# Layer 1's matrices into the states, built from loads that spread the input matrices and the turned powers over the partitions

## The chip, the cores and the metric

The kernel runs on one core of one Trainium2 chip. The metric is device time in microseconds (us), the median of several executions. One further execution was profiled; its trace is what the prediction reads.

## The reference, cut to what matters

Two layers of an encoder run over 256 tokens of width 1024. In each layer a normed input is projected to ten column groups; one branch is a bidirectional state-space model, two are attention, and the gated branches are projected back and added to the input. The change touches only the state-space branch, and in it only the matrices that carry a group's 16 input channels into its 64 complex states.

```python
for direction in range(2):
    lam_bar = exp(lam * dt)                       # per group (32) and state (64)
    b_bar = ((lam_bar - 1) / lam)[..., None] * b  # b is complex, (group, state, channel)
    bu = einsum('gpc,bsgc->bsgp', b_bar, u)
    h = scan(h[s] = lam_bar * h[s-1] + bu[s])     # direction 1 runs backwards
    y += einsum('gcp,bsgp->bsgc', c, h).real
```

The kernel cuts the 256 steps into 64 chunks of T = 4. A chunk's entry into the state is then one product: for step t of the chunk the matrix is b times the power of lam_bar that is left until the chunk's end. (The factor (lam_bar - 1) / lam is put on c instead.) So for each layer 128 rows (two directions x 64 states) x 32 groups x 16 channels x 4 steps of complex products b * q have to be formed, q being the four powers. On TensorE the contraction runs over (channel, step), so these must stand on the partitions, while powers and states are computed with (direction, state) on the partitions.

## The kernel before, in words

All work is written as streams (Python generators). A stream names the engine of its next step, the buffers that it needs and the events that it waits for. A planner (class Flow) keeps a modelled clock for each engine, gives every instruction a modelled cost, and always emits the step that can start first by its model, less a "patience" of its stream, with a "rank" to break ties. What comes out is one fixed order of instructions on each engine. The chip keeps that order: an instruction that waits holds back all that stand behind it on its engine. The planner's clocks run through the whole program, so a change in one step can give a different order of everything behind it, while what was emitted before it stays as it was.

SyncE (SP) issues nearly all DMAs, from one queue in the planned order. The weights come in pieces of 512 KB: load_pieces (L474) loads one into one of three raw slots, high_parts (L484) casts it on ScalarE (or VectorE) to whi (three slots), low_parts (L498) subtracts on VectorE to wlo (two slots), which frees the raw slot, and TensorE multiplies: 24 matmuls with 256 columns for a piece (run_layer, L1409, and mm3, L378). A raw load waits in SP's queue for its slot, and wlo waits for TensorE to be done with the piece two before. Almost every instruction is recorded under line 135, that of the planner's wrapper, so the names of the tiles tell the steps apart. If the planner sees a gap on TensorE, keep_warm (L432) lets it put small matmuls on an identity ("warm") there.

For each layer, ssm_params (L662) loads the parameters (layer 1 must wait for the slot "tab", which layer 0 holds until its last convolution matrices are computed), ssm_tables (L673) builds the powers pw and from them q1 (the four powers, in turned order for the backward direction), and ssm_into (L760) makes for each of four batches of eight groups the products wt on VectorE, five instructions of 512 elements per partition. into_turn (L788) then turns them: two groups of four TensorE transposes into a bank psw of PSUM ("sm", two banks for all small users), each followed by a ScalarE copy to wb. ssm_x (L803) multiplies wb with the inputs u into psx. Behind the end of layer 0 the norm, the splitting of the normed input and, through DRAM, the tiles xa, xad and u of layer 1 precede its first psx.

to_mix (L1249) is the step of layer 0 and 1 that gates the state-space output on VectorE (sg, mo, mix2) ahead of the last output products. DMA costs in the planner (L175): 0.475 us to issue (0.65 when a source with under 64 rows spreads over 128 partitions), 0.65 us to start, the bytes at 360 GB/s one DMA after another, 0.85 us to land.

Of the kernel before, what the change touches and what calls it, by code (L numbers as in the profile page):

```python
# [12 lines left out]
F32 = mybir.dt.float32  # L13
# [7 lines left out]
P = 128  # L21
# [5 lines left out]
HD = 64  # L27
GROUPS = 32
NST = 64
CH = 16  # L30
T = 4
# [3 lines left out]
NB = GROUPS // GB  # L35
N1 = NCH + 1
RS = GROUPS * N1
PAIRS = GB // 2
# [17 lines left out]


SLOTS = dict(raw=3, whi=3, wlo=2, act=3, qkv=6, g4=7, wb=4, tm=3, E=1, u=5, bias=2, t2k=2, pt=2, ptt=2,
            xa=1, sg=5, bd=1, bs=1, rs=1, ys=3, tab=1, atn=1, pj=3, sc=2, po=1, sm=2)

PLAIN = ((0, 1, 2, 3, 5, 8), (0, 1))

BY_DMA = (0, 0)

EARLY = (2, 1)
FILL = 0.9
# [18 lines left out]
            keep_x=(2.7, 8.1), pair=(2.5, 0.5), head=(2.5, 0.5), gelu=(9.0, 0.2), to_mix=(5.2, 1.4), to_x=(7.4, 1.4), load_pieces=1.5,  # L85
            into_turn=(0.1, 5.1), t5_rows=(1.9, 5.1), biases=(5.2, 7.9), reload_x=(1.3, 4.3),
            bias_glu=(8.7, 6.0), ssm_x=(3.8, 7.6), ssm_scan=(6.7, 3.1), ssm_kernels=(5.2, 4.9), ssm_y=(3.7, 3.6),
            ssm_up=(3.8, 3.1), ssm_tables=(2.1, 7.5), ssm_into=5.0, ssm_out=(0.8, 5.3), products=(5.2, 1.2))

BACKLOG = 4  # L90

# [12 lines left out]
def ap(base, offset, dims):  # L104
    return bass.AP(base.tensor, base.offset + offset, dims)


def free(t, offset, dims):

    return bass.AP(t.tensor, t.offset + offset, [t.ap[0]] + dims)  # L110
# [3 lines left out]
class Event:  # L114
    t, eng = None, None
# [225 lines left out]
def trunk(ctx: ExitStack, tc: tile.TileContext, io):  # L341
    nc = tc.nc
    flow = Flow(tc)
    V, A, G, PE, SP = flow.V, flow.A, flow.G, flow.PE, flow.SP

    sb = ctx.enter_context(tc.tile_pool(name="sb", bufs=1))
    dram = ctx.enter_context(tc.tile_pool(name="dram", bufs=2, space=DRAM))
    psum = ctx.enter_context(tc.tile_pool(name="psum", bufs=1, space=PSUM))

    def new(tag, dims, dtype=F32, name=None):  # L350

        return sb.tile([P] + dims, dtype, name=name or tag, tag=tag, bufs=SLOTS[tag])

    def bank(tag, name=None):
        return psum.tile([P, 512], F32, name=name or tag, tag=tag, bufs=SLOTS[tag])
# [1 line left out]
    def one(name, dims, dtype=F32, bufs=1):  # L357
        return sb.tile([P] + dims, dtype, name=name, tag=name, bufs=bufs)
# [28 lines left out]
    def events(n):  # L387
        return [Event() for _ in range(n)]
# [22 lines left out]
    ident, ones, epst = one("ident", [P]), one("ones", [1]), one("epst", [1])  # L411
    eye16, namask, fg = one("eye16", [CH]), one("namask", [2, NEAR]), one("fg", [KD])
    bd = one("bd", [2, GB, CH, 2])
# [259 lines left out]
    def ssm_tables(l, tb):  # L673

        G1 = GROUPS
# [8 lines left out]
        def rows(dst, first):  # L684
            A.copy(dst[:NST], pw[:NST, :, first:first + T, :])
            s = pw[NST:]
            A.copy(dst[NST:], free(s, (first + T - 1) * G1, [[STEP, 2], [-G1, T], [1, G1]]))

        for base, n in ((0, 1), (0, 2), (3, 1), (4, 1), (4, 2)):
            i = base + n  # L690
            yield "V", "tm"
            pt = new("tm", [2, 2, 2, G1], name="pt")
            pt1, pt2 = pt[:, 0], pt[:, 1]
            src = pw[:, :, base + 1:base + n + 1, :]
            V.tensor_mul(pt1[:, :, :n, :], src, free(pw, i * G1, [[0, 2], [0, n], [1, G1]]))
            yield "V"
            V.tensor_mul(pt2[:, :, :n, :], swapped(pw, (base + 1) * G1, STEP, [[G1, n], [1, G1]]),
                         free(pw, STEP + i * G1, [[0, 2], [0, n], [1, G1]]))
            yield "V"
            V.tensor_sub(pw[:, 0, i + 1:i + n + 1, :], pt1[:, 0, :n, :], pt2[:, 0, :n, :])  # L700
            V.tensor_add(pw[:, 1, i + 1:i + n + 1, :], pt1[:, 1, :n, :], pt2[:, 1, :n, :])
            flow.free("tm")
            if base == 0 and n == 2:

                yield "A"
                q1 = one("q1", [2, G1, T])
                rows(q1.rearrange("p r g t -> p r t g"), 0)
                q1sd = one("q1sd", [2, G1, T])
                yield "V"
                V.tensor_sub(q1sd[:, 0], q1[:, 0], q1[:, 1])  # L710
                V.tensor_add(q1sd[:, 1], q1[:, 0], q1[:, 1])
                tb.q1, tb.q1sd = q1, q1sd
                yield "V", tb.par_ev
                tb.bsum = one("bsum", [GROUPS, CH])
                V.tensor_add(tb.bsum, tb.bb[:, 0], tb.bb[:, 1])
                flow.set(tb.q1_ev)
# [39 lines left out]
        V.tensor_add(csum, cc[:, 0], cc[:, 1])  # L756
        tb.qc, tb.qsd, tb.csum = qc, qsd, csum
        flow.set(tb.ev)

    def ssm_into(l, tb):  # L760

# [258 lines left out]
    def ssm_start(l):  # L1020
        tb = Box()
        tb.wb, tb.wc, tb.toep, tb.y_left = [None] * NB, [], [None] * NB, NB
        tb.tab_ev, tb.par_ev, tb.q1_ev, tb.l_ev, tb.ev, tb.scan_ev, tb.wcs_ev = events(7)
        tb.into_ev, tb.x_ev, tb.wc_ev, tb.toep_ev = events(NB), events(NB), events(NB), events(NB)
        flow.spawn(ssm_params(l, tb), l)
        flow.spawn(ssm_tables(l, tb), l)
        flow.spawn(ssm_into(l, tb), l)
        return tb

    def ssm_run(L, tb):  # L1030
# [605 lines left out]
def layout(x, norm_g, w_in, w_out, ssm_lam_re, ssm_lam_im, ssm_log_dt, ssm_b_re, ssm_b_im, ssm_c_re, ssm_c_im,  # L1636
           ssm_d, glu_w, glu_b, na_rpb, t5_bias, final_g):
    a = {k: np.asarray(v) for k, v in locals().items()}
    L, G = DEPTH, GROUPS
    o = {}  # L1640
# [5 lines left out]
    w = a["w_in"]  # L1646
    w = np.concatenate([w[:, :, _SPLIT[i]:_SPLIT[i + 1]][:, :, pm if i == 1 else slice(None)] for i in _ORDER], axis=2)
# [11 lines left out]
    b = np.stack([a["ssm_b_re"], a["ssm_b_im"]], 1)  # L1659
    c = np.stack([a["ssm_c_re"], a["ssm_c_im"]], 1)  # L1660
    o["b_p"] = b.transpose(0, 2, 4, 1, 3, 5).reshape(L, P, 2, G, CH)
    o["c_p"] = c.transpose(0, 2, 5, 1, 3, 4).reshape(L, P, 2, G, CH)
    d = a["ssm_d"].reshape(L, 8, 4, CH)
    d = np.broadcast_to(d[..., None], (L, 8, 4, CH, 2))
# [22 lines left out]
```

## Time and profile before

| | us |
|---|---|
| Median of 3 executions | 459.48 (458.31 to 461.18) |
| The profiled execution | 457.03 |
| Its span, first to last instruction | 455.2 |
| TensorE busy | 444.5 (98%) |
| VectorE busy | 349.6 (77%) |
| ScalarE busy | 301.5 (66%) |
| DMA engines, mean share | 52% |

The span is what the trace covers; 1.8 us of the profiled execution lie around it. Busy time of TensorE counts pipelined matmuls, so it says that the engine had work, and the pace of the matmuls says how fast that went.

### The profile page before, as it was taken

The page shows a single profiled execution, that of the slowest core. Times are in us where ns is not written, and L with a number is a line of the kernel's source. Part 1 is how long each engine was busy: PE and PEld are TensorE (multiplying, and loading weights), DVE is VectorE, ACT ScalarE, POOL GpSimd, SP SyncE. Part 2 cuts the span into 40 slices and gives each one's busy share as a digit, 9 for nine tenths or more (in the row PEclk, how much of TensorE's full clock was granted, in tenths as well). Part 3 has the DMA queues.
Part 4 walks back from the last instruction along what each step waited for, and adds up shares of the span by engine and source line. Part 5 has one row for each costly group of instructions (what it writes and reads, how often), then busy time and mean ns, then how long its engine had stood idle before and what let it go on. Part 6 is the DMA issues. An engine that isn't in the chain of part 4 may idle for free.

```text
span 455.2 us, 11299 instructions
## 1 busy us (share of the span) xinstructions
PE 444.5 (98%) x4484; PEld 412.4 (91%) x4484; DVE 349.6 (77%) x747; ACT 301.5 (66%) x607; POOL 30.6 (7%) x61
## 2 busy tenths in 40 slices
PE   8999999998999999999999999999999999999994
PEld 7779899788888999999998999998998999999994
DVE  5899979998798688879728889499899654468533
ACT  6444889784687866846534687967787793756532
POOL 1020031210000000000000110232000000000000
PEclk9999999999999999999999999999999999999998
DMA  7755362545767344545626844755564654554503
GB/s 261 247 176 194 103 193 77 146 134 161 275 186 225 123 137 144 175 159 179 212 110 199 245 146 124 195 152 167 174 192 144 204 169 130 195 182 151 177 1 93
DMA packets 46005, 75.79 MB, mean 166 GB/s; under 512 B 20944, under 2 KB 29264, under 8 KB 45952
## 3 DMA queue, kind: packets, MB, share of 16 engines
q1 hardware_dynamic: 45808, 74.97, 52.3%
q8 instruction: 35, 0.57, 0.5%
q14 instruction: 18, 0.15, 0.1%
q10 hardware_dynamic: 144, 0.10, 0.1%
HBM read 70.38 MB, written 4.67 MB: 165 GB/s over the span
## 4 chain that ended last, share of the span: by engine, by line
PE 78%; DVE 9%; DMA 6%; ACT 3%; issue 1%; SPq 1%; POOL 0%; DVEq 0%; ACTq 0%; POOLq 0%
PE pj L135 58%; PE psy L135 4%; PE po L135 3%; PE sc L135 3%; PE psx L135 3%; PE pp L135 3%; DMA xad<-xa 2%; DMA raw<-w_in 2%; PE psn L135 2%; PE psw L135 2%; DMA xin<-x 1%; DMA bias<-rpb 1%; PE psr L135 1%; DVE t1s L135 1%; DVE wlo L135 1%
## 5 line engine op out<-in xcount | busy, mean ns | idle before, releaser
L135 DVE TENSOR_TENSOR wlo<-raw,whi 128x1024 fp32r<-128x1024 f32 x92 | 113.9, 1238 | 44.7 <-PE pj L135 25.5
L135 ACT CAST whi<-raw 128x1024 fp32r<-128x1024 f32 x92 | 96.1, 1046 | 63.1 <-PE pj L135 39.8
L135 PE MATMUL pj<-h0h,whi 128*128 128x256 f32 x192 | 57.2, 298 | 0.0
L135 PE MATMUL pj<-h1h,whi 128*128 128x256 f32 x192 | 56.2, 292 | 0.0
L135 PE MATMUL pj<-h0l,whi 128*128 128x256 f32 x192 | 54.3, 283 | 0.0
L135 PE MATMUL pj<-h1h,wlo 128*128 128x256 f32 x192 | 54.2, 283 | 0.0
L135 PE MATMUL pj<-h0h,wlo 128*128 128x256 f32 x192 | 54.2, 283 | 0.0
L135 PE MATMUL pj<-h1l,whi 128*128 128x256 f32 x192 | 54.2, 282 | 0.0
L135 POOL TENSOR_TENSOR bias<-bias,namask 128x160 f32<-128x160 f32 x32 | 25.6, 802 | 214.7 <-DMA bias<-rpb 177.3
L135 PEld LDWEIGHTS pj<-h0h,whi 128*128 128x128 f32 x192 | 36.7, 191 | 2.2 <-issue 1.9
L135 PEld LDWEIGHTS pj<-h1h,whi 128*128 128x128 f32 x192 | 36.7, 191 | 1.5 <-issue 1.2
L135 PEld LDWEIGHTS pj<-h0h,wlo 128*128 128x128 f32 x192 | 36.7, 191 | 0.1
L135 PEld LDWEIGHTS pj<-h1h,wlo 128*128 128x128 f32 x192 | 36.7, 191 | 0.0
L135 PEld LDWEIGHTS pj<-h1l,whi 128*128 128x128 f32 x192 | 36.7, 191 | 0.0
L135 PEld LDWEIGHTS pj<-h0l,whi 128*128 128x128 f32 x192 | 36.6, 191 | 0.0
L135 PE MATMUL pj<-xin,raw 128*128 128x256 f32 x128 | 31.4, 385 | 0.2 <-DVE xin L135 0.2
L135 ACT ACTIVATE pt<-pt,nm 128x160 f32<-128x160 f32 (+1 forms) x64 | 29.5, 463 | 0.8 <-DVE nm L135 0.7
L135 ACT ACTIVATE pt<-pt,sm 128x256 f32<-128x256 f32 (+1 forms) x62 | 26.9, 465 | 3.6 <-DVE sm L135 3.5
L135 PEld LDWEIGHTS pj<-xin,raw 128*128 128x128 f32 x128 | 22.9, 190 | 4.4 <-DVE xin L135 1.3
L135 ACT COPY E<-psx 64x512 f32<-64x512 f32 x32 | 18.6, 580 | 7.4 <-PE psx L135 6.9
L135 ACT COPY ptt<-pp 128x512 f32<-128x512 f32 x32 | 18.7, 585 | 6.8 <-PE pp L135 6.6
L135 PE MATMUL pj<-gx,raw 128*128 128x256 f32 x96 | 22.4, 384 | 0.0
(196 smaller groups left out, 1201.7 us busy)
## 6 DMA issues: line engine op xcount, KB each, us to landing
raw<-w_in SPq DMA_DIRECT2D x78, 512.0 KB, 3.7
raw<-w_out SPq DMA_DIRECT2D x24, 512.0 KB, 3.2
bias<-vdram SPq DMA_DIRECT2D x16, 192.0 KB, 3.4
raw<-glu_w SPq DMA_DIRECT2D x4, 512.0 KB, 3.1
bias<-rpb SPq DMA_DIRECT2D x16, 120.0 KB, 3.9
xin<-x SPq DMA_DIRECT2D x4, 256.0 KB, 5.2
raw<-w_in SPq DMA_DIRECT2D x4, 256.0 KB, 4.9
cc<-c_p SPq DMA_DIRECT2D x2, 512.0 KB, 6.4
```

The lines of the kernel that those rows point to most:

```text
L135: return f(*args, **kw)
```

## The change

Layer 0 stays as it is. In layer 1 q1 is written with the group as its innermost index. turned_powers transposes it on TensorE (two transposes into one bank), copies it to SBUF and writes it by two DMAs to a DRAM tile qd, split into even and odd groups. ssm_into_rows takes the place of ssm_into and into_turn. It goes in eight rounds, two for each batch. A round loads bt (256 KB: layer 1's b with (parity of the group, channel) on the rows, each row read four times so that it stands on 128 partitions) from a new input b_t that the host lays out, and two halves qt of 64 partitions (128 KB each, every row of qd read 16 times); both have one buffer each, taken at the round's start and freed at its end. Four VectorE instructions, two of 512 and two of 256 elements per partition, form the complex product directly in wb. q1sd, bsum, wt, the 32 transposes psw and the eight copies of psw are gone from layer 1. The load of b_p stays, since the convolution matrices use it.

```diff
--- before.py
+++ after.py
@@ -56,11 +56,13 @@
 
 
 SLOTS = dict(raw=3, whi=3, wlo=2, act=3, qkv=6, g4=7, wb=4, tm=3, E=1, u=5, bias=2, t2k=2, pt=2, ptt=2,
-            xa=1, sg=5, bd=1, bs=1, rs=1, ys=3, tab=1, atn=1, pj=3, sc=2, po=1, sm=2)
+            xa=1, sg=5, bd=1, bs=1, rs=1, ys=3, tab=1, atn=1, bt=1, pj=3, sc=2, po=1, sm=2)
 
 PLAIN = ((0, 1, 2, 3, 5, 8), (0, 1))
 
 BY_DMA = (0, 0)
+
+BY_ROWS = (False, True)
 
 EARLY = (2, 1)
 FILL = 0.9
@@ -85,7 +87,7 @@
             keep_x=(2.7, 8.1), pair=(2.5, 0.5), head=(2.5, 0.5), gelu=(9.0, 0.2), to_mix=(5.2, 1.4), to_x=(7.4, 1.4), load_pieces=1.5,
             into_turn=(0.1, 5.1), t5_rows=(1.9, 5.1), biases=(5.2, 7.9), reload_x=(1.3, 4.3),
             bias_glu=(8.7, 6.0), ssm_x=(3.8, 7.6), ssm_scan=(6.7, 3.1), ssm_kernels=(5.2, 4.9), ssm_y=(3.7, 3.6),
-            ssm_up=(3.8, 3.1), ssm_tables=(2.1, 7.5), ssm_into=5.0, ssm_out=(0.8, 5.3), products=(5.2, 1.2))
+            ssm_up=(3.8, 3.1), turned_powers=5.0, ssm_into_rows=5.0, ssm_tables=(2.1, 7.5), ssm_into=5.0, ssm_out=(0.8, 5.3), products=(5.2, 1.2))
 
 BACKLOG = 4
 
@@ -347,9 +349,9 @@
     dram = ctx.enter_context(tc.tile_pool(name="dram", bufs=2, space=DRAM))
     psum = ctx.enter_context(tc.tile_pool(name="psum", bufs=1, space=PSUM))
 
-    def new(tag, dims, dtype=F32, name=None):
-
-        return sb.tile([P] + dims, dtype, name=name or tag, tag=tag, bufs=SLOTS[tag])
+    def new(slot, dims, dtype=F32, name=None, tag=None):
+
+        return sb.tile([P] + dims, dtype, name=name or slot, tag=tag or slot, bufs=SLOTS[slot])
 
     def bank(tag, name=None):
         return psum.tile([P, 512], F32, name=name or tag, tag=tag, bufs=SLOTS[tag])
@@ -704,6 +706,10 @@
 
                 yield "A"
                 q1 = one("q1", [2, G1, T])
+                if BY_ROWS[l]:
+                    rows(free(q1, 0, [[GROUPS * T, 2], [G1, T], [1, G1]]), 0)
+                    flow.spawn(turned_powers(tb, q1), l)
+                    continue
                 rows(q1.rearrange("p r g t -> p r t g"), 0)
                 q1sd = one("q1sd", [2, G1, T])
                 yield "V"
@@ -756,6 +762,54 @@
         V.tensor_add(csum, cc[:, 0], cc[:, 1])
         tb.qc, tb.qsd, tb.csum = qc, qsd, csum
         flow.set(tb.ev)
+
+    def turned_powers(tb, q1):
+
+        yield "PE", "sm"
+        ps = bank("sm", "psq")
+        for ri in range(2):
+            PE.transpose(ps[:, ri * P:(ri + 1) * P], q1[:, ri].rearrange("p g t -> p (g t)"), ident)
+        yield "A", "ys"
+        qt = new("ys", [2 * P], name="qt")
+        A.copy(qt, ps[:, :2 * P])
+        flow.free("sm")
+        yield "SP"
+
+        tb.qd = dram.tile([T, 2, NB * PAIRS, 2 * P], F32, name="qd", bufs=1)
+        for r in range(2):
+            dma(tb.qd[:, r], qt[r::2])
+        flow.free("ys")
+        flow.settle()
+        flow.set(tb.qd_ev)
+
+    def ssm_into_rows(l, tb):
+
+        n = PAIRS // 2
+        for b in range(NB):
+            for i in range(2):
+                yield ("SP", "bt", tb.qd_ev)
+                bt, qt = (new("bt", [n, 2, P], name=x, tag=x) for x in ("bt", "qt"))
+                o = (b * PAIRS + i * n) * 2 * P
+                dma(bt, ap(io["b_t"], l * 2 * CH * NB * PAIRS * 2 * P + o, [[NB * PAIRS * 2 * P, 2 * CH], [0, T], [1, n * 2 * P]]))
+                for r in range(2):
+                    if r:
+                        yield "SP"
+                    dma(qt[HD * r:HD * r + HD], ap(tb.qd, r * NB * PAIRS * 2 * P + o,
+                                                  [[0, CH], [2 * NB * PAIRS * 2 * P, T], [1, n * 2 * P]]))
+                yield ("V", "g4", "wb") if i == 0 else "V"
+                if i == 0:
+                    w = new("g4", [PAIRS, 2, P], name="wb")
+                wi = w[:, i * n:(i + 1) * n]
+                V.tensor_mul(wi, bt, qt)
+                yield "V"
+                V.tensor_mul(bt, bt, free(qt, P, [[2 * P, n], [-P, 2], [1, P]]))
+                yield "V"
+                V.tensor_add(wi[:, :, 0], wi[:, :, 0], wi[:, :, 1])
+                yield "V"
+                V.tensor_sub(wi[:, :, 1], bt[:, :, 0], bt[:, :, 1])
+                flow.free("bt")
+            tb.wb[b] = w
+            flow.set(tb.into_ev[b])
 
     def ssm_into(l, tb):
 
@@ -1020,11 +1074,11 @@
     def ssm_start(l):
         tb = Box()
         tb.wb, tb.wc, tb.toep, tb.y_left = [None] * NB, [], [None] * NB, NB
-        tb.tab_ev, tb.par_ev, tb.q1_ev, tb.l_ev, tb.ev, tb.scan_ev, tb.wcs_ev = events(7)
+        tb.tab_ev, tb.par_ev, tb.q1_ev, tb.l_ev, tb.ev, tb.scan_ev, tb.wcs_ev, tb.qd_ev = events(8)
         tb.into_ev, tb.x_ev, tb.wc_ev, tb.toep_ev = events(NB), events(NB), events(NB), events(NB)
         flow.spawn(ssm_params(l, tb), l)
         flow.spawn(ssm_tables(l, tb), l)
-        flow.spawn(ssm_into(l, tb), l)
+        flow.spawn((ssm_into_rows if BY_ROWS[l] else ssm_into)(l, tb), l)
         return tb
 
     def ssm_run(L, tb):
@@ -1659,6 +1713,7 @@
     b = np.stack([a["ssm_b_re"], a["ssm_b_im"]], 1)
     c = np.stack([a["ssm_c_re"], a["ssm_c_im"]], 1)
     o["b_p"] = b.transpose(0, 2, 4, 1, 3, 5).reshape(L, P, 2, G, CH)
+    o["b_t"] = b.reshape(L, 2, 2, NB, PAIRS, 2, NST, CH).transpose(0, 5, 7, 3, 4, 1, 2, 6).reshape(L, 2 * CH, -1)
     o["c_p"] = c.transpose(0, 2, 5, 1, 3, 4).reshape(L, P, 2, G, CH)
     d = a["ssm_d"].reshape(L, 8, 4, CH)
     d = np.broadcast_to(d[..., None], (L, 8, 4, CH, 2))
```

## Rows read from the trace of the kernel before

**Rows 1.** The page: its span, and TensorE's busy tenths in 40 slices.
```profile
span 455.2 us, 11299 instructions
...
PE   8999999998999999999999999999999999999994
```

**Rows 2.** Stretches (us): busy time and instructions of each engine, clock, DMA share, GB/s.
```profile
157.00:182.00 25.00, 25.00 (x330) 24.44 (x329) 21.95 (x33) 16.61 (x22) 0.15 (x1) 1.00 0.43 140
182.00:204.00 22.00, 22.00 (x187) 22.00 (x186) 17.50 (x31) 14.75 (x24) 0.00 (x0) 1.00 0.49 169
204.00:214.00 10.00, 10.00 (x86) 10.00 (x85) 9.32 (x15) 7.19 (x11) 0.00 (x0) 1.00 0.47 157
214.00:236.00 22.00, 22.00 (x181) 21.79 (x180) 11.96 (x16) 10.21 (x20) 0.00 (x0) 1.00 0.55 192
236.00:264.00 28.00, 27.21 (x248) 24.64 (x247) 21.69 (x39) 15.39 (x32) 3.32 (x6) 1.00 0.66 193
```

**Rows 3.** TensorE in order of time around one psw group: start, us, instruction.
```profile
164.89 0.28 PE L135 MATMUL pj<-h0l,whi 128*128 128x256 f32 x1
165.01 0.60 PE L135 MATMUL psw<-ident,wt 128*128 128x128 f32 x4
165.37 0.36 PE L135 MATMUL pj<-h0h,whi 128*128 128x256 f32 x1
165.57 0.28 PE L135 MATMUL pj<-h0h,wlo 128*128 128x256 f32 x1
```

**Rows 4.** The tile psw, both layers: durations in ns, first and last start.
```profile
L135 PE MATMUL psw<-ident,wt x64: 271/272/273, 32.9 to 185.7; 128*128 128x128 f32 x64
L135 ACT COPY wb<-psw x16: 579/588/593, 33.6 to 187.7; 128x512 f32<-128x512 f32 x16
```

**Rows 5.** Groups by form, both layers: busy us, mean ns | idle before.
```profile
L135 DVE TENSOR_TENSOR wt<-bb,q1sd 128x512 f32<-128x512 f32 x16 | 10.9, 692 | 0.0
...
L135 DVE TENSOR_TENSOR ys<-ys,psy 128x256 f32<-128x256 f32 x8 | 3.4, 420 | 6.1 <-ACT ys L135 6.0
```

**Rows 6.** VectorE in order of time in one batch of the products.
```profile
162.12 0.69 DVE L135 TENSOR_TENSOR wt<-tmi,wt 128x512 f32<-128x512 f32 x1
162.72 0.68 DVE L135 TENSOR_TENSOR wt<-wt,tmi 128x512 f32<-128x512 f32 x1
```

**Rows 7.** DMA issues by tile: count, KB each, median us to landing.
```profile
raw<-w_out SPq DMA_DIRECT2D x24, 512.0 KB, 3.2
...
xad<-xa SPq DMA_DIRECT2D x8, 128.0 KB, 2.2
...
toep<-rd SPq DMA_DIRECT2D x32, 32.0 KB, 3.1
...
yT<-yd SPq DMA_DIRECT2D x16, 64.0 KB, 3.2
```

**Rows 8.** SP's queue from 155 to 240 us, longest wait: us, times, longest.
```profile
SPq L135 <- DVE wlo L135: 41.8, 19, 3.4
```

**Rows 9.** VectorE in order of time: subtractions wlo in the gating stretch.
```profile
204.34 1.22 DVE L135 TENSOR_TENSOR wlo<-raw,whi 128x1024 fp32r<-128x1024 f32 x1 [0.39 <-issue]
...
208.80 1.22 DVE L135 TENSOR_TENSOR wlo<-raw,whi 128x1024 fp32r<-128x1024 f32 x1
```

**Rows 10.** TensorE in order of time: first use of those two, and warm matmuls.
```profile
207.20 0.28 PE L135 MATMUL pj<-mix0h,wlo 128*128 128x256 f32 x1
...
209.96 0.39 PE L438 MATMUL warm<-ident 128*128 128x128 f32 x2
...
210.31 0.28 PE L135 MATMUL pj<-mix1h,wlo 128*128 128x256 f32 x1
```

**Rows 11.** A stretch of 4 us at the start of layer 1, columns as in group 2.
```profile
248.00:252.00 4.00, 3.95 (x45) 3.56 (x44) 2.68 (x4) 1.49 (x3) 0.00 (x0) 1.00 0.98 298
```

**Rows 12.** The chain of waits in order of time: start, us, what.
```profile
256.90 5.40 DMA raw<-w_in
```

**Rows 13.** TensorE in order of time: layer 1's first product into the states.
```profile
249.79 2.00 PE L135 MATMUL psx<-u,wb 64*128 64x64 f32 x32
```

## The prediction

> **What bounds the kernel now.** I began with the page. TensorE is busy in nine tenths or more of all but the first and the last slice [rows 1], so the question is whether it works at its pace or only looks busy, and which engine would be next. The table by stretches answers the second part for the time that the change touches: from 157 to 236 us TensorE is idle in no stretch, its clock is at full grant (1.00, the 2.4 GHz level), VectorE has 3.05 of 25 us free at 157 to 182, 4.5 of 22 at 182 to 204, 0.68 of 10 at 204 to 214 and 10 of 22 after that, and the DMA engines are half used [rows 2]. The timeline of TensorE answers the first part: matmuls of 256 columns start 0.12 us apart, and where the four transposes of a psw group come between them, the next matmul starts 0.36 us after the group and the one behind it 0.20 us later [rows 3]. The turning of layer 1's products is therefore on the path. VectorE's share of it is beside it, with one narrow place, below. Reading the chain of waits alone would have told less, since it follows TensorE through this time.
>
> **Part by part: TensorE.** A psw group costs 0.36 + 0.20 - 0.12 = 0.44 us of matmul time [rows 3]. Of the 64 transposes half are layer 1's, eight groups, the last beginning about 185.7 us [rows 4], all in the stretches where TensorE is never idle [rows 2]. That removes 8 x 0.44 = 3.5 us. The two transposes of turned_powers put back half a group and its restart, 0.18 + 0.08 = 0.26 us. Net -3.3 us on the path.
>
> **ScalarE.** Eight copies of psw go, 8 x 0.588 = 4.7 us [rows 4], and one copy of half the size comes. ScalarE has over 7 us free in each of the three longer stretches of the 79 us [rows 2], so I cost this at nothing; the cover is its own idle time, and it can only get longer.
>
> **VectorE.** A product of 512 elements takes 0.692 us, one of 256 takes 0.420 [rows 5], and two that follow each other start 0.60 us apart [rows 6]. Layer 1 loses 20 products and the sum bsum at the first price and two small ones, about 21 x 0.69 + 0.5 = 15.0 us; it gains 16 x 0.692 + 16 x 0.420 = 17.8 us. The work grows by 2.8 us and moves: now 20 products lie from 158 to 182 us, afterwards eight rounds follow each other, each bound by its own loads.
>
> **Where the rounds fall.** The powers are ready at about 157 us. Transposes, copy and the DMAs to qd (like xad, 2.2 us [rows 7]) bring the first load to about 162. A round moves as many bytes as one weight piece, which lands 3.2 us after its issue [rows 7], but with three issues ahead of the last landing I take 4.2. Four instructions take 2 x 0.60 + 2 x 0.42 = 2.0 us. A round's loads also stand in SP's queue behind raw loads that wait for their slot, 41.8 us in 19 waits [rows 8], 2.2 us each; half of one per round is 1.1. Waiting for VectorE between other instructions costs one subtraction at most, 1.2 us [rows 9]; half is 0.6. In all 8 us a round, 64 us for eight: from 162 to 226 us. Layer 1's first product into the states starts at 249.8 [rows 13] and needs only the first two rounds, so the longer way costs nothing there: the cover is over 20 us even for the last round, and would be gone only at 11 us a round.
>
> **The narrow place.** Between 204 and 214 us to_mix stands on VectorE between the subtractions. The wlo that begins at 204.34 ends 1.6 us before its first use at 207.20; the next ends at 210.02 and is used at 210.31, 0.3 us later, and the planner had already put warm matmuls there [rows 9, 10]. A round's 2.0 us in this stretch go straight into TensorE's time. At 8 us a round, one or two rounds fall into ten microseconds: 2.0 to 4.0 us if all of it counts, 0 if the planner, which favours to_mix by its patience of 0.339 against the round's 0, puts the round's instructions in other gaps (0.68 us are free there [rows 2]) and moves table work behind 214. I take 1.0, nearer to the low end, because the two streams compete by that patience and the stretch behind it has 10 us of room.
>
> **DMA.** SP gets 26 more issues of 0.4 to 0.6 us, about 13 us in 64, and the DMA engines 4 MB of loads, 65 GB/s on top of 157 to 192 [rows 2]. The nearest row for a crowded queue is the start of layer 1: at a share of 0.98 and 298 GB/s TensorE was still busy 3.95 of 4.00 us [rows 11], though soon after a weight piece took 5.40 us instead of 3.2 to land [rows 7, 12]. A crowded queue at its worst loses 0.79 us of TensorE in 28 [rows 2], which is 1.8 in 64. So 0 to 1.8 us, and I take 0, because the expected 220 to 260 GB/s stay below that row. The case where it does more is a rival.
>
> The two halves qt are where a rule speaks against the change. The nearest row, yT<-yd in halves of 64 partitions, takes 3.2 us to land for 64 KB, where xad<-xa over 128 partitions takes 2.2 for 128 KB [rows 7]; but the former gathers short rows and the latter writes to DRAM, so this is no clean comparison. The Trainium skill (SBUF — State Buffer, "Can I just issue two DMAs to hit both halves?" and the section on the port swizzle before it) says that 64 partitions reach only half the ports and that two such transfers one after the other don't add up, and gives 196 GB/s for one. By an estimate from that figure each half would take 0.67 us and a round's loads would land 0.6 us later than at full width. Eight rounds would end at 231 instead of 226 us, which costs nothing; a round in the narrow place would hold VectorE 0.6 us longer, and the sum below would be -1.7 instead of -2.3 us.
>
> **Sum.** -3.3 + 1.0 = -2.3 us. Against the profiled execution, 457.03 us, this is 454.7. That execution is 2.45 us under the median of the runs, so the median goes from 459.48 to **457.2**. The terms' bounds are -3.3 to +2.5 (-3.3 + 4.0 + 1.8), 456.2 to 462.0. The runs shown spread by 0.6%, and with that and a new order of instructions I take 1% as what tells a change of this kernel from none.
>
> **Rival 1: the plan around layer 1 gets tighter.** The new plan differs from 157 us on. TensorE's idle time from 236 to 264 us is 0.79 us [rows 2], and the warm matmuls at 209.96 hold 0.14 us of pace [rows 10]. If those go too and no round hits the narrow place, the gain is 3.3 + 0.9 = 4.2 us, 455.3; the spread of three runs (1.2 us below the median) can make it 454.1. That is the only way to over 1%, since TensorE is idle almost nowhere else before the end. For it: the rounds leave 157 to 182 freer. Against: it needs every term at its best.
>
> **Rival 2: rounds block VectorE and the weights starve (slower).** VectorE keeps its order, so a round's first product that stands ahead of a wlo holds it until bt and qt have landed. The planner counts on 0.65 + 2 x 0.475 us of issues and about 2.0 us for bytes and landing, 3.6 in all. By rows it is 4.2, and with a queue as crowded as at 256.90 it is 5.4 plus 1.0 of earlier issues, 6.4 [rows 7, 12]; a load behind a raw wait of 3.4 us that the planner did not foresee adds that [rows 8]. The cover is the wlo's margin, 1.6 us by the first of the two rows, 0.3 by the second [rows 9, 10]. It decides once a round is over 1.6 us later than planned. With a mean lateness of 2.8 to 3.0 us eight rounds lose 8 x 1.3 = 10.4, and the raw loads issued behind the bursts come late as well, which the same stall hides. -3.3 + 10.4 = +7.1: 466.6. For it: one buffer each and no prefetch, VectorE 88% busy at 157 to 182 [rows 2]. Against: DMA is half used and SP's waits come from the same slots that the planner models.
>
> **Rival 3: the saving turns into filler.** If VectorE's narrow place, and not TensorE, sets when layer 0's last products start, the 3.3 us are spent as more warm matmuls near 210 us and nothing is left: 459.5, or 461 if a round falls there too. For it: margins of 0.3 us and the warm rows [rows 9, 10]. Against: VectorE waits for TensorE before that place, so it moves forward with it.
>
> **That the change doesn't do what it says** would be products that still pass through TensorE; the code leaves only two transposes, so I give it no chance of its own.
>
> **How the numbers follow.** Forecast, -3.3 to about +1 us: 0.47. Rival 1: 0.20, all of it counted as faster by over 1%. Rival 3 and small reorderings within 1%: 0.15. Rival 2: 0.18, slower by over 1%. So faster 0.20, same 0.62, slower 0.18. The range for 8 in 10 leaves out the best third of rival 1 and the worse half of rival 2: 453.8 to 465.5. The forecast's own is 456.2 to 460.5.
>
> **What would show it.** In the profile after: psw only for layer 0 (32 transposes), TensorE at 0.12 us a matmul from 162 to 200 us with no idle time, and the end of layer 0's input projections about 3 us earlier; bt and qt loads from about 162 us, eight rounds of 7 to 9 us, the last before 240; VectorE's share up by some 3 us in all. Rival 2 shows as VectorE idle in front of the first product of a round, released by a DMA, with a wlo and then TensorE late behind it; rival 3 as more warm matmuls around 207 to 213. I am wrong if TensorE has new idle time between 160 and 235 us of more than 2 us, if the rounds reach into 250 us, or if layer 1, from its first psx on, takes some us longer than before for an order that this change only disturbed.

## The result, and the profile after

The changed kernel is slower: 466.94 us (median of 4, 465.18 to 467.41) against 460.33 us for the kernel before on the same chip (4 runs, 458.31 to 461.50), a ratio of 1.0141 with the interval 1.0093 to 1.0189. The forecast was 457.2, with a range that ended at 465.5. Here and below a ratio leaves out executions far above their kernel's fastest, so it need not be the quotient of the medians beside it.

The page after, to be laid beside [rows 1]: its span, then one of its rows over 40 slices. PEclk is TensorE's granted clock in tenths.

```profile
span 464.9 us, 11322 instructions
...
PEclk9999999999999999999999979999999999999995
```

The span is 9.7 us longer than in the profile of before, of which about 3 us belong to that one execution (457.03 against a median of 460.33 here; the profiled execution after took 466.94). Two slices show what is new: a clock below 9 in the middle (about 267 to 279 us) and a lower clock in the last slice.

The table by stretches after, columns and stretches as in [rows 2]:

```profile
157.00:182.00 25.00, 25.00 (x328) 24.39 (x327) 18.12 (x30) 15.96 (x26) 0.15 (x1) 1.00 0.64 194
182.00:204.00 22.00, 20.44 (x166) 19.63 (x165) 17.26 (x27) 10.85 (x15) 0.00 (x0) 1.00 0.57 181
204.00:214.00 10.00, 10.00 (x86) 10.00 (x85) 9.13 (x15) 6.04 (x10) 0.00 (x0) 1.00 0.73 242
214.00:236.00 22.00, 22.00 (x185) 21.92 (x184) 14.16 (x20) 10.04 (x18) 0.00 (x0) 1.00 0.68 223
236.00:264.00 28.00, 26.51 (x241) 23.87 (x239) 22.61 (x43) 14.63 (x29) 1.14 (x2) 1.00 0.67 192
```

From 182 to 204 us TensorE is now idle for 1.56 us, and VectorE does no more work than before (17.26 against 17.50 us). So it isn't the amount of VectorE's work; something stands in front of it. The chain of waits from 176 to 195 us says what (start, us, what; only some of its long pieces are shown):

```profile
176.29 6.78 DMA qt<-qd
...
183.19 0.70 DVE wb L137
...
187.84 4.46 DMA qt<-qd
...
192.38 0.70 DVE wb L137
...
194.59 0.59 DVE mix1l L137
```

Loads of the turned powers lead the chain, then a round's products, and behind them what layer 0's output needs: mix1l. TensorE in order of time there (in brackets: idle before, and what ended it):

```profile
189.81 0.39 PE L137 MATMUL pj<-mix1l,whi 128*128 128x256 f32 x1 [0.22 <-DVE mix1l L137]
...
191.11 3.07 PE L440 MATMUL warm<-ident 128*128 128x128 f32 x26
193.93 0.36 PE L137 MATMUL pj<-mix1h,whi 128*128 128x256 f32 x1
...
195.25 0.39 PE L137 MATMUL pj<-mix1l,whi 128*128 128x256 f32 x1 [0.84 <-DVE mix1l L137]
```

The 26 warm matmuls are filler: the planner itself saw that mix1l would come 3 us late. They count as busy, so the stretch's 20.44 us of busy time hide them; only 17.4 us of it are work. Then mix1l comes 0.84 us later still, because VectorE had to wait for a load (below). The way to the end, as starts of the same instruction before and after: a po product ahead of the changed work 145.86 and 145.46 (-0.4), first mix0 product 189.36 and 185.87 (-3.5), mix0 behind mix1 195.56 and 196.55 (+1.0), first psn of layer 0's end 219.0 and 220.6 (+1.6), first psx of layer 1 249.79 [rows 13] and 252.26 (+2.5), third psx group 273.18 and 280.36 (+7.2), layer 1's first psn 423.9 and 431.9 (+8.0), span +9.7. The 0.4 us at po stood there before the change acts. From there on 3.1 us were won, 5 lost again by 220 us, and the start of layer 1 lost 6 more.

VectorE in order of time where layer 0 hands over to layer 1, after:

```profile
238.56 0.69 DVE L137 TENSOR_TENSOR wb<-bt,qt 128x512 f32<-128x512 f32 x1 [2.71 <-DMA qt<-qd]
239.17 0.16 DVE L137 RECIPROCAL nr<-nr 128x2 f32<-128x2 f32 x1
...
241.30 0.88 DVE L137 SCALAR_TENSOR_TENSOR x<-x,ng,rstd 128x256 f32<-128x256 f32 x2
```

The seventh round's product stands ahead of the norm's reciprocal and waits 2.71 us for its load; x is scaled at 241.30, before at 238.25. Later a weight piece lands 5.4 us after its issue, and TensorE stands still (the second line waits for rs, which follows a ScalarE copy that stood behind that piece's cast):

```profile
266.27 0.43 PE L137 MATMUL psx<-u,wb 64*128 64x64 f32 x2
268.49 1.80 PE L137 MATMUL psx<-u,wb 64*128 64x64 f32 x22 [1.79 <-DVE rs L137]
```

and the clock falls behind it (stretches, columns as above; the granted clock is the third number from the end). By an estimate from these rows, (0.32 + 0.50 + 0.03) x 4 us, the clock costs 3.4 us here:

```profile
264.00:268.00 4.00, 2.70 (x20) 2.43 (x20) 2.00 (x4) 1.43 (x4) 1.99 (x4) 1.00 0.73 278
268.00:272.00 4.00, 3.51 (x33) 3.42 (x34) 3.31 (x7) 2.00 (x5) 0.00 (x0) 0.68 0.63 180
272.00:276.00 4.00, 4.00 (x21) 4.00 (x20) 3.05 (x3) 2.77 (x5) 0.00 (x0) 0.50 0.30 79
276.00:280.00 4.00, 4.00 (x90) 3.83 (x89) 2.25 (x5) 2.63 (x7) 0.00 (x0) 0.97 0.35 116
```

The waits of VectorE after, 157 to 255 us (us in all, times, longest), and the loads after (count, KB each, median us to landing):

```profile
DVE wb L137 <- DMA qt<-qd: 7.0, 4, 2.7
```

```profile
bt<-b_t SPq DMA_DIRECT2D x8, 256.0 KB, 5.1
qt<-qd SPq DMA_DIRECT2D x16, 128.0 KB, 5.3
```

These four waits come to 7.0 us. The planner counts 2.9 us from a bt issue to its landing: 0.65 to issue, 0.65 to start, 0.73 for the bytes, 0.85 to land. The shortest was 4.8 us for bt and 4.3 for qt, and half of the rounds held VectorE.

### The profile page after: what moved, and what is told of

Same layout as the page of the kernel before. It is cut to its first block, busy times and chain, and to the rows that moved or that the text cites. A ratio compares the mean times of both kernels' runs of the same rounds, so it can differ in the third digit from the quotient of the medians.

```text
span 464.9 us, 11322 instructions
## 1 busy us (share of the span) xinstructions
PE 451.4 (97%) x4478; PEld 418.5 (90%) x4478; DVE 353.8 (76%) x757; ACT 298.2 (64%) x599; POOL 29.6 (6%) x61
## 4 chain that ended last, share of the span: by engine, by line
PE 70%; DMA 12%; DVE 10%; ACT 2%; SPq 2%; issue 2%; DVEq 0%; ACTq 0%
PE pj L137 51%; DMA qt<-qd 4%; PE po L137 3%; PE sc L137 3%; PE psx L137 3%; PE psy L137 3%; PE pp L137 3%; DMA raw<-w_in 3%; SPq L137 2%; DVE wlo L137 2%; DVE wb L137 1%; DMA gb<-glu_b 1%; DMA xin<-x 1%; PE psn L137 1%; DMA yd<-ys 1%
## 5 line engine op out<-in xcount | busy, mean ns | idle before, releaser
L137 POOL TENSOR_TENSOR bias<-bias,namask 128x160 f32<-128x160 f32 x32 | 24.6, 768 | 214.5 <-DMA bias<-rpb 210.8
L137 ACT ACTIVATE pt<-pt,sm 128x160 f32<-128x160 f32 (+1 forms) x61 | 26.1, 462 | 4.4 <-DVE sm L137 4.2
```

The costliest lines, as they stand in the source:

```text
L137: return f(*args, **kw)
```

## The experiments

The letters in the expectations are four theories about the loss. **A**: the loads land later than the planner counts, and since VectorE keeps its order, a round's first product holds everything behind it. **B**: 26 more issues and 4 MB cost as such, in the queue and on the way. **C**: any new order of this tuned plan costs some us. **D**: TensorE arrives some 3 us early at products whose gating VectorE does late, since the planner puts the rounds ahead of it; the saving is spent as filler. Each run was compared with the kernel before on its own chip. In the runs "gating ahead" means one number, to_gate's patience, which makes the planner emit the gating earlier.

**Prefetch alone.** bt and qt of a round share a buffer of the pool g4, two rounds can be in flight, and products have streams of their own.

```diff
...
-                yield ("SP", "bt", tb.qd_ev)
+                yield ("SP", "bt", "g4", tb.qd_ev)
+                t = new("g4", [2, n, 2, P], name="btqt")
+                bt, qt = t[:, 0], t[:, 1]
...
+                flow.spawn(rows_products(tb, b, i, bt, qt, here), l)
...
```

> The loads of up to two rounds are in flight: each round's bt and qt share one g4 buffer and a stream of their own forms the products, so a round's loads are issued while the round before is still computed. Theory A (the rounds' loads land later than the planner counts on, VectorE holds wlo behind them, TensorE starves): the waits of VectorE for qt, 7.0 us in the changed kernel, fall under 2 us, TensorE's idle time between 182 and 204 us (1.56 us) goes, and the time is 456 to 461 us. Theory B (the added loads and issues as such make the weights late): the same 4 MB are loaded in less time, so 464 to 470 us. Theory C (any new order of the instructions costs some us): 460 to 470 us, with no tie to the waits.

Measured 462.49 us (10 runs), ratio 1.0039 (1.0002 to 1.0077). Two thirds of the loss are gone, but VectorE still waits 6.2 us in three waits, and TensorE runs 36 warm matmuls from 190.61 ahead of mix1. Layer 1's first psx comes no earlier than in the changed kernel (253.17 and 252.26 us); from there to layer 1's first psn it takes 173.8 us, as before (174.1), where the changed kernel takes 179.7. Prefetch takes the loss at the start of layer 1 and leaves D's.

**The lateness told to the planner.** One line behind the loads:

```diff
+                flow.cur.pend += 2.5
```

> The changed kernel, but the planner counts on the loads of a round landing 2.5 us later, close to what the trace shows (5.1 us after issue instead of 2.9 for bt). Loads and instructions are the same, only the planned order differs. Theory A: VectorE's waits for qt fall under 2 us and with them the stalls, 458 to 463 us. Theory B: 465 to 469 us, as the changed kernel. Theory C: anything from 460 to 470.

Measured 462.22 us (10 runs), ratio 1.0032 (0.9997 to 1.0068). Same buffers, same loads, same traffic, and 1.1% of the 1.4% are gone: no wait of VectorE for bt or qt is left. Filler is left: 20 warm matmuls (2.40 us) at 189.51. For A, against B.

**The loads left out.** Only the first round loads; the seven others multiply that same tile, so their matrices are not the model's.

```diff
+                if b or i:
+                    yield "V"
+                else:
+                    yield ("SP", "bt", tb.qd_ev)
...
```

> The changed kernel with the loads of the first round alone; the other seven rounds compute on what is in the buffers, so 21 of the 24 loads are left out and the matrices are not those of the reference. Theory A: no late loads are left and TensorE has 3.3 us less to do than before the change: 456 to 460 us. Theory B: the same, 456 to 460. Theory C: 460 to 468, since the order is new here too. So this run tells A and B from C.

Measured 469.47 us (4 runs), ratio 1.0194 (1.0113 to 1.0274): without any load to wait for, the slowest kernel of all. A and B alone can't explain this. The chain of waits of this run:

```profile
179.96 8.52 PE pj L137 x71
188.48 12.51 PE warm L440 x112
200.99 4.07 PE pj L137 x34
```

and VectorE in order of time:

```profile
189.60 0.68 DVE L137 TENSOR_TENSOR wb<-bt,qt 128x512 f32<-128x512 f32 x1
...
197.75 0.43 DVE L137 TENSOR_TENSOR wb<-bt 128x256 f32<-128x256 f32 x1
198.09 1.29 DVE L137 TENSOR_TENSOR atn<-thz,atn 128x512 f32<-128x512 f32 x2
```

With nothing to wait for, four rounds stand in one block from 189.60 to 198.1 us ahead of atn, and TensorE fills 12.5 us. That is D by itself: the planner lets the rounds pass the gating whenever they can go first.

**The loads alone.** The kernel before, transposes and all, with eight rounds of loads that nothing needs (24 of the change's 26 issues; the two writes of qd are not among them, and qt's halves are read from b_t); two tiny copies per round wait for them on VectorE.

```diff
...
+            yield "V"
+            V.tensor_copy(one("got", [2]), bt[:, 0, 0, :2])
+            V.tensor_copy(one("got", [2]), qt[:, 0, 0, :2])
...
```

> The kernel before the change (layer 1's products and transposes as they were), with eight rounds of three loads of the changed kernel's sizes added, which nothing needs: two small VectorE copies end each round. Theory A: the loads alone cost little, since only small instructions wait for them, and those can still hold VectorE's queue: 459 to 464 us. Theory B: the 4 MB and 24 issues are what costs, 466 to 471 us. Theory C: a new order, 459 to 468.

Measured 466.08 us (4 runs), ratio 1.0114 (1.0041 to 1.0187). VectorE's waits, 157 to 240 us:

```profile
DVE got L138 <- DMA qt<-b_t: 6.6, 4, 3.0
DVE got L138 <- DMA bt<-b_t: 2.2, 2, 2.1
```

This is most of the loss without any of the change's arithmetic. It doesn't yet tell a wait (A) from traffic (B); the last run does.

**The gating ahead, alone and as a control.** One number, in the changed kernel and in the kernel before:

```diff
-            to_gate=(-0.225, 0), ...
+            to_gate=(0.3, 0), ...
```

> The changed kernel, in which layer 0's gating (atn, then mix1) gets a patience of 0.3 instead of -0.225, so that the planner puts it ahead of the rounds on VectorE; loads and instructions are the same. In the changed kernel layer 0's first output product starts 3.5 us earlier than before, and TensorE then spends 26 warm matmuls and waits until mix1 comes from VectorE. Theory D (the saved time runs into VectorE's chain atn, mix1, which the rounds hold back, and is gone there; the late rounds then cost again at the start of layer 1): the warm matmuls between 185 and 200 us fall under 6, the second half of mix1 is used 2 to 4 us earlier than 195 us, and the time is 461 to 464 us, the cost at the start of layer 1 being left. Theory A (late loads): the waits for qt are the same, so 465 to 468 us.

> The kernel before the change with the same patience for the gating. Theory D: there the gating stands behind the products too, but the transposes keep TensorE busy meanwhile, so there is little to win: 458 to 461 us, the same as before within its spread. If a new order as such costs time (theory C): 463 us or more.

The changed kernel with it: 467.32 us (6 runs), 1.0182 (1.0135 to 1.0229), a miss for D. The filler is gone (4 warm matmuls), but VectorE's waits for loads grew to 9.2 us in five. The control: 460.04 us (12 runs), 1.0006 (0.9973 to 1.0039), so the number by itself neither wins nor loses, and C has nothing to stand on there.

**One round of loads and the gating ahead.** The kernel with the loads left out, with that number.

> The changed kernel with the loads of the first round alone (21 of 24 left out, so the matrices are not the reference's) and the gating ahead. Without the second edit it took 469.5 us, and its trace shows 112 warm matmuls, 12.5 us, while TensorE waits for mix1. Theory D: those are gone, no load is late, and the 3.3 us of TensorE are gained: 455 to 459 us. If it stays at 464 us or more, what the rounds cost is neither loads nor gating.

Measured 458.30 us (12 runs) against 460.29, ratio 0.9995 (0.9959 to 1.0031); with the gating behind, the ratio was 1.0194. So about 2%, 9 us, of that kernel were order. Its profiled execution, the fastest of its twelve (452.78 us), has the saving all along: po at 145.18 us instead of 145.86, g2 at 197.55 instead of 201.32, the span 451.0 instead of 455.2, so 3.1 to 3.5 us won behind po. The medians lie 2.0 us apart and the ratio shows no gain at all; why the two differ isn't settled.

**Prefetch and the gating ahead.**

> The loads of two rounds in flight and the gating ahead of the products. Theories A and D together: both causes are out of the way, 456 to 460 us, as fast as the kernel before the change or up to 1% faster. Theory B (4 MB and 26 issues as such): 461 to 465 us, no better than with the prefetch alone (462.5).

Measured 460.23 us (12 runs), ratio 0.9965 (0.9923 to 1.0008): the loss is gone, no gain is shown. VectorE still waits 5.6 us for loads.

**The loads alone, the gating ahead.**

> The kernel before with the rounds' loads added (26 issues, 4 MB, two tiny copies on VectorE per round that wait for them) and the patience that lets layer 0's gating stand ahead; the transposes stay on TensorE, so no time is saved. It closes the table of loads, saving and order. Theory A (a late load holds VectorE at its place in the order, whatever the order is): about the time of the loads alone, 464 to 467 us, since nothing of the loads changes. Theory D (only the order of the rounds against the gating costs): 459 to 461, as the kernel before, because the gating no longer waits behind the rounds. Both together: A's number here, since the saving that D needs is absent.

Measured 465.86 us (4 runs), ratio 1.0159 (1.0096 to 1.0223), A's number. VectorE's waits, 157 to 255 us:

```profile
DVE got L138 <- DMA qt<-b_t: 6.7, 4, 2.8
DVE got L138 <- DMA bt<-b_t: 1.0, 1, 1.0
```

With the order of the gating changed, the loads-only kernel is no faster. The four runs spread from 462.36 to 469.88, so more than that they don't show.

**The lateness told and the gating ahead.**

> The changed kernel, with the planner told that a round's loads land 2.5 us later than it counts, and with the patience that lets layer 0's gating stand ahead. Each of the two alone gave 462.2 and 467.3 us. If the two causes interlock (A: loads that land later than planned hold VectorE; D: rounds ahead of the gating hold the products), both are out of the way and the time is that of the prefetched variant with the same patience or a little less, 457 to 461 us, with the products of mix1 starting within 0.5 us of the end of mix0. If the loads cost as traffic in the queues (B), it stays at 464 or more, with weight pieces late all through 160 to 240 us.

Measured 461.64 us (10 runs), ratio 1.0044 (1.0011 to 1.0077), 0.6 us above what was expected. Up to layer 1's first psx the profile has what the theories say: mix0 at 185.14, mix1 at 188.16, g2 at 197.26, psx at 246.11 instead of 249.79. But with one buffer and loads planned at their length the last round comes at 297.4 us, the fourth psx group at 300.3 instead of 283.5, and layer 1's first psn at 424.6 instead of 423.9. So between layer 1's first psx and its first psn 4.4 us are lost. The trace shows part of it: TensorE stands idle for 1.54 us of 252 to 256 us, at the second psx group, for a load of u and a ScalarE copy E, and the granted clock is 0.67 and 0.91 in the two stretches of 4 us behind, where it was 1.00 before. By an estimate from these two, (0.33 + 0.09) x 4 us, the clock costs 1.7 us. What the rest is, isn't shown.

**All three: prefetch, the lateness told, the gating ahead.** One line more than in the run of prefetch and gating:

```diff
                 here = Event()
+                flow.cur.pend += 2.5
                 flow.set(here)
```

> Prefetch of one round (bt and qt of a round in one buffer, two rounds in flight, products in streams of their own), the lateness of 2.5 us told to the planner, and the patience that lets the gating stand ahead. A with D: VectorE waits for no load longer than 1 us, layer 0's last products start 3 to 4 us earlier than in the kernel before, and the time is 455 to 459 us, below the kernel before by up to 1%. B (the traffic itself): 460 us or more, as with prefetch and patience alone.

Measured 456.35 us (10 runs, 453.88 to 459.11) against 459.72, ratio 0.9916 (0.9883 to 0.9948): faster than both kernels, and the only version shown faster than the kernel before. TensorE in order of time where the changed kernel had its filler:

```profile
191.00 0.39 PE L440 MATMUL warm<-ident 128*128 128x128 f32 x2
191.14 0.36 PE L137 MATMUL pj<-mix1h,whi 128*128 128x256 f32 x1
```

and its loads from 157 to 240 us:

```profile
raw<-w_out SPq DMA_DIRECT2D x12, 512.0 KB, 4.9
...
btqt<-b_t SPq DMA_DIRECT2D x8, 256.0 KB, 5.5
btqt<-qd SPq DMA_DIRECT2D x16, 128.0 KB, 5.5
```

The loads land later than in the changed kernel (5.5 against 5.1 and 5.3 us), the weights too (4.9 against 4.0), and it is about 10 us faster by the ratios: no instruction of VectorE waits for one of the rounds' loads. The profiled execution, the slowest of the ten (459.11 us, span 457.3 against 455.2), shows where the gain lies and what hides it there: po begins 1.8 us later than before (147.70), layer 0's first psn 1.4 us earlier (217.66), layer 1's first psn 1.6 us earlier (422.33), so 3.2 and 3.4 us are won behind po; behind that the clock falls to 0.50, and from the first psn to the end it takes 35.0 us instead of 31.3.

**The loads alone, the lateness told.** The loads-only kernel, its copies in a stream of their own with the same 2.5 us.

> The kernel before with the same added loads as in the run of the loads alone (26 issues, 4 MB, two tiny copies per round), but the planner is told that they land 2.5 us later than it counts and each round's copies stand in a stream of their own. TensorE's order differs from the loads-only kernel's by a few lines. Theory A (what costs is VectorE standing in front of a load that is late): 459 to 462 us, VectorE's waits for these loads under 1 us in all, and the weights on time. Theory B (26 issues and 4 MB cost as such): 464 to 467 us, as with the loads alone, with weight pieces landing later between 157 and 240 us. A time in between splits the cost.

Measured 460.77 us (10 runs) against 460.55, ratio 1.0021 (0.9983 to 1.0058). The stretch 182 to 204 us of the two loads-only kernels, first as it was, then with the lateness told:

```profile
182.00:204.00 22.00, 19.82 (x149) 19.00 (x148) 16.93 (x36) 12.20 (x17) 0.00 (x0) 0.92 0.74 220
```

```profile
182.00:204.00 22.00, 22.00 (x187) 22.00 (x186) 17.83 (x36) 15.26 (x25) 0.00 (x0) 1.00 0.69 219
```

The same 219 to 220 GB/s, the loads landing after 4.7 and 4.8 us (4.7 and 4.6 in the first), and TensorE goes from 2.2 us idle to none, its granted clock from 0.92 to 1.00. B falls: the bytes and issues by themselves cost nothing that these runs can show (up to 0.6% lies within the interval).

The ratios together:

| | gating behind | gating ahead |
|---|---|---|
| transposes, no loads | 1 | 1.0006 |
| transposes, loads | 1.0114 | 1.0159 |
| transposes, loads, lateness told | 1.0021 | not run |
| no transposes, one round of loads | 1.0194 | 0.9995 |
| the change | 1.0141 | 1.0182 |
| the change, lateness told | 1.0032 | 1.0044 |
| the change, prefetch | 1.0039 | 0.9965 |
| the change, prefetch and lateness told | not run | 0.9916 |

Apart from 1.0194, each loss of over 1% belongs to a kernel with one buffer for the loads whose planner counts on them early; telling it the lateness takes the loss below 0.5%, and so does prefetch. The sum of VectorE's waits doesn't decide: with prefetch it still waits 6.2 and 5.6 us (7.0 in the changed kernel), at 1.0039 and 0.9965. What a wait costs depends on what stands behind it. The gating's place decides alone only where no load delays the rounds (1.0194 to 0.9995); with late loads and one buffer it gains nothing. A gain is shown only with all three. How much of it is the gating can't be read from these runs, since the corner with prefetch and lateness told, gating behind, wasn't run.

## Why the prediction was wrong

**TensorE, -3.3 us: right.** psw is left in layer 0 alone. TensorE in order of time, before, then after:

```profile
145.86 1.08 PE L135 MATMUL po<-ptt,v 128*64 128x256 f32 x8
...
189.36 0.28 PE L135 MATMUL pj<-mix0h,whi 128*128 128x256 f32 x1
```

```profile
145.46 1.08 PE L137 MATMUL po<-ptt,v 128*64 128x256 f32 x8
...
185.87 0.28 PE L137 MATMUL pj<-mix0h,whi 128*128 128x256 f32 x1
```

From po to the first mix0 product it takes 3.1 us less, and as much less in six of the eight other versions that have the change. Counting from such a common instruction matters: the profiled executions begin po up to 1.8 us away from the one of before, ahead of everything that the change touches.

**ScalarE, nothing: right** as far as it goes. **VectorE, +2.8 us of work:** over the 107 us of [rows 2] its busy time is 81.3 us after and 82.4 before, so the added work didn't come due there as a sum; over the whole span it is 4.2 us more (353.8 against 349.6). Neither size matters beside the waits.

**Where the rounds fall: the step that failed.** A round's loads were put at 4.2 us to land and the round at 8 us, with over 20 us of cover and a limit of 11. Measured: 5.1 and 5.3 us for a single load to land, 5.7 to 8.8 us from a round's first issue to its first product where VectorE stood waiting for it, and the first product of a round 11.2 us behind that of the round before on average (170.2 us for the first, 248.3 for the eighth, seven steps). Of these 11.2 us, 7.8 lie between a round's first issue and its first product, where the text had 4.2. The other 3.4, from there to the next round's first issue, are about what it had (3.7 for the products, the waits between them and SP's queue). So the loads are the term that was too small. The first load was issued at 162.3 us, as forecast. The cover was gone, as the text had said it would be at that pace: round seven stood in front of layer 1's norm, and round eight ended at 252.2 us, one of the signs that the text had named. Worse than the size was the use made of it: lateness was charged to the rounds' own end. The sum has no term for what stands behind a round's first product on VectorE, only rival 2 has one, though the planner's number and mine differed already (3.6 and 4.2). The runs showed in its place 7.0 us of VectorE's time in four waits, which the run with the lateness told takes away with most of the loss (1.0141 to 1.0032).

**The narrow place: the wrong place.** It was looked for at 204 to 214 us, where TensorE was busy 10.00 of 10.00 us before and after. It was at 189 to 195 us. The trace of before shows it, in lines that the prediction didn't read; VectorE, then TensorE, before the change:

```profile
192.32 1.23 DVE L135 TENSOR_TENSOR wlo<-raw,whi 128x1024 fp32r<-128x1024 f32 x1 [0.42 <-PE pj L135]
193.46 0.69 DVE L135 TENSOR_TENSOR mix1l<-atn,mix1h 128x512 fp32r<-128x512 f32 x1
```

```profile
194.36 0.29 PE L135 MATMUL pj<-mix1l,whi 128*128 128x256 f32 x1
```

mix1l ends at 194.15 and is used at 194.36, 0.2 us later. VectorE after the change:

```profile
190.28 1.22 DVE L137 TENSOR_TENSOR wlo<-raw,whi 128x1024 fp32r<-128x1024 f32 x1
192.38 0.69 DVE L137 TENSOR_TENSOR wb<-bt,qt 128x512 f32<-128x512 f32 x1 [0.88 <-DMA qt<-qd]
...
194.51 0.69 DVE L137 TENSOR_TENSOR mix1l<-atn,mix1h 128x512 fp32r<-128x512 f32 x1
```

So the argument against rival 3, that VectorE waits for TensorE ahead of the narrow place and moves with it, held as far as the wlo: it waited 0.42 us for TensorE before and comes 2.0 us earlier now. What undid it is the round that the planner put between that wlo and mix1l. The stream that makes atn and mix1 there is to_gate, whose patience of -0.225 ranks it behind the round's 0; the prediction had weighed the rounds against to_mix's 0.339 alone. In the run of all three, where that number is 0.3, both halves of mix1l are done at 190.1 us, ahead of their first use at 191.56.

**DMA, 0 to 1.8 us, 0 taken: right** for traffic as such, within the last run's interval and by the fastest one. By the Trainium skill (SBUF — State Buffer, "Can I just issue two DMAs to hit both halves?") two half transfers don't add up; here a half of 128 KB took 5.3 us to land and the full-width 256 KB 5.1, which fits the estimate's direction, but no run loaded qt in one piece.

**Rival 2 is what happened**, at 466.6 against 466.94 measured, by the mechanism that it named: VectorE idle in front of a round's first product, released by a DMA, the weights and TensorE late behind. Its sum was not how the time was lost: four waits, 7.0 us in all, not eight rounds of 2.8 to 3.0, then layer 1's start and its clock. That the two numbers agree is luck. It was given 0.18 for two reasons against it. "DMA is half used" was true of before (0.43 to 0.55) and not of after (0.57 to 0.73 from 157 to 236 us). "SP's waits come from the same slots that the planner models" was beside the point: the landing is what the planner doesn't model.

**Rival 3** was right as a mechanism, 3.07 us of warm matmuls, but not as an end: it came on top of rival 2 instead of in its place. The two were given as alternatives, and they share one cause, rounds ahead of other work on an engine that keeps its order.

## What to carry to other kernels

A load that feeds an in-order engine is priced by what stands behind its first reader, not by its own bytes: where it may land later than the plan says, give it a buffer ahead and a pessimistic landing time before anything else is counted. Time saved on the bounding engine is real only up to the next product whose operand another engine makes with a margin smaller than the saving, unless that engine moves with it and nothing new is put in between, so read those margins all along the path, not at one place. Filler counts as busy: look for it by name before believing a full engine.

## What the runs showed of the hardware

**Loads land late well below full load.** At a DMA share of 0.57 to 0.73, pieces of 128 to 256 KB took 4.3 to 6.7 us to land and weight pieces 4.0 us in the median instead of 3.2 [rows 7]; with more in flight 5.5 and 4.9. The other rounds' traffic isn't needed for it: in the two kernels that load one round alone, the halves took 5.4 to 5.7 and 4.6 us. What of it is the loads' shape and what the queue, no run here separates.

**The clock fell after 1.79 us of idle time.** TensorE was idle 1.30 us of 264 to 268 and 0.49 of the next 4 us, and the granted clock went to 0.50 (the 1.2 GHz level) for the whole of 272 to 276, where it was busy all the time. Before, 264 to 280 us had 15.66 of 16 us busy and a clock of 1.00.

**It also fell where the table shows no idle time.** Near the end after the change, stretches as above:

```profile
452.00:456.00 4.00, 4.00 (x28) 4.00 (x28) 1.06 (x5) 1.62 (x5) 0.00 (x0) 0.72 0.00 0
456.00:460.00 4.00, 3.97 (x19) 3.67 (x18) 1.93 (x6) 1.03 (x4) 0.00 (x0) 0.50 0.45 131
```

Of the fourteen profiled executions three kept 1.00 to their last products (before, the one round of loads with the gating ahead, the loads alone with the lateness told); the other eleven fell to the 1.2 GHz level 6 to 12 us ahead of them, the control too, which has the work of before and a span of 458.5 us against 455.2. What sets it off, no run here tells. Layer 1's first psn and the span's end stand 31.3 us apart before and 33.0 after: 1.7 of the 9.7 us between the two profiles.
